# The whole depthwise convolution on TensorE, with weights spread by the host, and the weight splits of the second block on VectorE

## The chip, the cores and the metric

One core of a Trainium2 chip. TensorE (PE in the profile) multiplies and transposes, VectorE (DVE), ScalarE (ACT) and GpSimd (POOL) work element by element, SyncE (SP) issues the DMAs, 16 DMA engines move the data. The metric is device time of one execution in microseconds, the median of several runs; lower is better.

## The reference

Two transformer blocks on one sequence of 256 positions and width 1024, in float32. The first block (a hybrid attention mixer and a SwiGLU FFN, closed by an RMS norm) is not touched. The second, cut to what matters:

```python
h = rms_norm_2(x, norm1_g)
q, k, v, a, g = jnp.split(h @ w_in, splits, axis=-1)         # 512 wide each
attn = neighbourhood_attention(q, k, v, rpb)
conv = conformer_conv(a, g, conv_w, conv_b, conv_ln_g, conv_ln_b)
mixed = concat([rms_norm_2(attn, attn_out_g), rms_norm_2(conv, conv_out_g)])
x = x + mixed @ w_out
h = rms_norm_2(x, norm2_g)
x = x + expert_choice_ffn(h, w_router, w_gate, w_up, w_down) # 16 experts, 1024 -> 2048 -> 1024
return rms_norm_2(x, final_g)

def conformer_conv(a, gate, ...):
    u = a * sigmoid(gate)
    dw = depthwise_conv(u, conv_w) + conv_b    # 31 taps over positions, 512 channels, each by itself
    return silu(layer_norm(dw, ln_g, ln_b))
```

## The kernel before, in words

**Splits.** A linear layer works on float32 weights in slabs of 128x1024. `split()` (L278 on) makes of each slab a high part `wh` (ScalarE, L287) and a low part `wl` = slab minus `wh` (L288, on VectorE or, where the table `POOLS` names the slab, on GpSimd). `linear_steps()` asks for the splits of a layer and then issues, per slab and row half, six products: high with high and low, low with high, of two k each (L249). A product can't start before its `wh` or `wl` is there.

**The second block.** Five linears read `w_b[0..4]`: the first two give the GLU halves of the conv (`ev_glu(n)`; its product `th`, L963, is transposed on TensorE and copied into `upad`), then q, k and v. The out projection `w_o2` has a part for the conv (`mixC`) and, at the end, one for the attention (`mixA`). The first linear begins while the first block's last slabs leave (`leave`, tiles `raw` and `xg`). The 31 taps of the 512 channels run in four chunks of 128 channels:
- chunk 0 on VectorE, 31 operations on `acc[:, 0]` (L1008, L1010);
- chunk 1 on ScalarE (product) and GpSimd (sum, L1024);
- chunks 2 and 3 on TensorE (`conv_pe`): `upad` goes to DRAM (`udram`), comes back as `u4`, four copies of 32 channels shifted by one position (four DMAs a chunk), and 32 small products a chunk take four taps each. Their spread weights `wst` are built on the core from `conv_wq` and `sumsel`, by GpSimd and by VectorE.

`swish` then transposes `acc`, takes the LayerNorm (`BN_STATS`, `z`) and the swish, and makes `mixC`. `scores` and `values` are the attention (`e`, `pt`, `on`, `mixA`). The router and the experts follow.

**What sets the order.** Every part is a generator that yields either a time or the marks that it needs. `weave` (L233) runs the flow that is due first by a clock of its own, that counts the products issued; TensorE follows this order as written, the other engines run in the order of their queues. SP's queue issues nearly all DMAs, in order: one that waits for a slot holds all behind it.

**Loads ahead.** Twelve slots of 2 MB hold one expert's weights (`in_e_g`, `in_e_u`, `in_e_d`, some as two halves). Four `e_g` slots of the first expert load during the FFN of the first block, at the slabs in `AH`, into the pools of `turns`; the others as the second block frees them. The loads of the next expert reuse them one by one, when TensorE has read them.

Of the kernel before, what the change touches and what calls it, by code (L numbers as in the profile page):

```python
# [9 lines left out]
FT = mybir.dt.float32  # L10
# [3 lines left out]
AF = mybir.ActivationFunctionType  # L14
OP = mybir.AluOpType
# [29 lines left out]
_columns(PRM, [("iota", 32), ("nhalf", 16), ("n2_g", 8), ("fin_g", 8)])  # L45
_columns(PR2, [("sumsel", 32), ("ffn_g", 8), ("out_g", 8), ("conv_w", 62), ("conv_wq", 64), ("conv_b", 4), ("w_r", 128)])

# [10 lines left out]
def _arrays(i):  # L58
# [28 lines left out]
    put("n2_g", _cols(i["norm2_g_2"][0]))  # L87
    cw = i["conv_w_2"][0]
    put("conv_w", cw[:, :256].T.reshape(2, 128, 31).transpose(1, 0, 2))
    cw = np.concatenate([cw[:, 256:], np.zeros((1, 256), np.float32)])  # L90
    put("conv_wq", cw.reshape(8, 4, 2, 4, 32).transpose(1, 4, 2, 3, 0))
    put("conv_b", _cols(i["conv_b_2"][0]))
# [42 lines left out]

POOLS = [[], [1, 3], [1, 3], [1, 3], [1, 3], [1, 3], [1, 3], [0, 1, 3], [1, 3], [1, 3], [], [], [], [3], [3], [3], [2, 3], [3], [3], [3], [2, 3], [3], [3], [2, 3], [], [1, 3], [1, 3], [1, 3]]
AH = [2, 4, 7, 8]
ORDERS = [(0, 0, 0, 1, 0, 1, 1, 1), (0, 0, 0, 0, 1, 1, 1, 1), (0, 0, 1, 0, 0, 1, 1, 1), (0, 0, 0, 1, 1, 0, 1, 1), (0, 0, 1, 0, 1, 0, 1, 1), (0, 1, 0, 0, 1, 0, 1, 1)]
# [6 lines left out]
def _program(nc, tc, A, dbg=None):  # L145
# [84 lines left out]
    def mark(name, after=0.0):  # L230
        marks[name] = clock[0] + after
# [77 lines left out]

    def linear_steps(slot, xt, evac, n=512, gcol=None, mid=None, ks=range(8), turn=None, fine=False, pool=False):  # L310

        us = sorted({k // 2 for k in ks})
        on, order_ = (range(8), 0) if pool else next(settings)
        turn = turn or ORDERS[order_]
# [544 lines left out]

    ahead = []  # L860
    turns = [[ringh] * 2, [ringx], [ringb], [ringb]]

    def feed():
        prev = []
        for b in range(11):
# [90 lines left out]
    def ev_glu(n):  # L956
        def ev(t, ps):
# [45 lines left out]
    def conv_dve():
        yield "u00", "u01"
        for k in range(31):
            u, w = upad[:, 0, k:k + 256], cw[:, 0, k:k + 1]
            if k == 0:
                V.tensor_scalar(acc[:, 0], u, w, cb[:, 0:1], op0=OP.mult, op1=OP.add)  # L1008
            else:
                V.scalar_tensor_tensor(acc[:, 0], u, w, acc[:, 0], op0=OP.mult, op1=OP.add)  # L1010
            if k % 3 == 2:
                yield 2.48
        mark("conv0", 4.72)

    def conv_act():
        yield "u00", "u01"
        for k in range(31):
            u, w = upad[:, 1, k:k + 256], cw[:, 1, k:k + 1]
            if k == 0:
                S.activation(acc[:, 1], u, AF.Identity, bias=cb[:, 1:2], scale=w)  # L1020
            else:
                o = be.tile([128, 256], FT, tag="prod", name="prod", bufs=2)
                S.activation(o, u, AF.Identity, scale=w)
                G.tensor_tensor(acc[:, 1], acc[:, 1], o, op=OP.add)  # L1024
            if k % 3 == 2:
                yield 0
        mark("conv1", 2.96)


    udram = dram.tile([2, 128, 288], FT, name="udram")  # L1030

    def conv_pe():
        wq = pp("conv_wq").rearrange("p (c a g) -> p c a g", c=2, g=8)
        sumsel = pp("sumsel")[:, None, :].to_broadcast([128, 8, 32])
        wst = be2.tile([128, 4, 8, 32], FT, tag="wst", name="wst")
        with tc.issue_after(last_pow[0]):
            for j in range(4):
                G.tensor_tensor(wst[:, j], wq[:, 0, j, :, None].to_broadcast([128, 8, 32]), sumsel, op=OP.mult)
        yield "u10", "u11"
        for c in range(2):  # L1040
            u4 = be2.tile([128, 4, 284], FT, tag="u4", name="u4")
            for r in range(4):
                nc.sync.dma_start(out=u4[32 * r:32 * r + 32], in_=udram[c, :, r:r + 284].rearrange("(j i) s -> i j s", i=32))
            yield 8.16
            ps = bank("sc")
            for g in range(8):
                for j in range(4):
                    MM(ps[32 * j:32 * j + 32, :256], wst[:, j, g], u4[:, j, 4 * g:4 * g + 256], g == 0, g == 7)
                if g % 2:
                    yield 0  # L1050
            S.activation(acc[:, 2 + c], ps[:, :256], AF.Identity, bias=cb[:, 2 + c:3 + c])
            if c == 0:
                wst = be2.tile([128, 4, 8, 32], FT, tag="wst", name="wst")
                for j in range(4):
                    V.tensor_tensor(wst[:, j], wq[:, 1, j, :, None].to_broadcast([128, 8, 32]), sumsel, op=OP.mult)
        mark("conv2", 0.81)

# [106 lines left out]
    def block():  # L1164
# [299 lines left out]
```

## Time and profile before

| | us |
|---|---|
| median of three runs | 1457.74 |
| lowest, highest | 1454.93, 1458.69 |
| the profiled execution | 1459.36 |
| its span in the profile | 1456.6 |
| TensorE busy | 1119.6 (77%) |
| VectorE busy | 443.5 (30%) |
| GpSimd busy | 165.7 (11%) |

Times in the profile are microseconds from the start of the span. A row of the time order gives start, duration, engine, line, operation, out<-in and, in brackets, how long the engine was idle before it and what ended that. Rows that follow one another with the same names are drawn together (x18 are eighteen instructions).

### The profile page before, as it was taken

To read this page: it belongs to the slowest core of one execution; us is meant where nothing else is said; L and a number is where in the kernel's file an instruction comes from. 1 tells how busy PE (TensorE), PEld (TensorE's weight loads), DVE (VectorE), ACT (ScalarE), POOL (GpSimd) and SP (SyncE) were. 2 spreads that over 40 slices of the span, in tenths; PEclk is the share of its full clock that TensorE was granted. 3 is DMA by queue.
4 is the path that set the end of the run, shared out by engine and by line. 5 is a ranking of instruction groups with operands and counts; after the bars stand their busy time and mean duration, and the time that the engine had idled before them with its cause. 6 is when DMAs were issued, how large, how long until landed. Compare 5 with 4: busy or idle time off the path is not lost.

```text
span 1456.6 us, 15371 instructions
## 1 busy us (share of the span) xinstructions
PE 1119.6 (77%) x6323; PEld 562.7 (39%) x6323; DVE 443.5 (30%) x819; ACT 332.2 (23%) x610; POOL 165.7 (11%) x119
## 2 busy tenths in 40 slices
PE   6989999999998898765675665677666667676575
PEld 5867877888876684111211111121111121111112
DVE  6576676445589542100110010001000011011002
ACT  5455646445576631000000000000000000000001
POOL 4433200100048530000000000000000000000001
PEclk9999999999999899888788788877778878878879
DMA  8623256757454578999999999999999999999997
GB/s 299 254 107 116 87 202 238 279 209 294 165 188 146 196 296 346 427 429 429 430 429 427 430 430 428 431 427 430 431 425 430 431 428 428 428 430 429 428 429 295
DMA packets 50598, 494.65 MB, mean 340 GB/s; under 512 B 5857, under 2 KB 7649, under 8 KB 10721
## 3 DMA queue, kind: packets, MB, share of 16 engines
q1 hardware_dynamic: 50528, 493.69, 82.3%
q8 instruction: 49, 0.80, 0.2%
q14 instruction: 21, 0.16, 0.0%
HBM read 492.32 MB, written 1.34 MB: 339 GB/s over the span
## 4 chain that ended last, share of the span: by engine, by line
DMA 63%; PE 24%; DVE 9%; ACT 2%; issue 1%; SPq 0%; POOL 0%; POOLq 0%; ACTq 0%; DVEq 0%
DMA slot<-in_e_g 18%; DMA half<-in_e_d 15%; PE mm L249 14%; DMA half<-in_e_g 8%; DMA half<-in_e_u 7%; DMA slot<-in_e_u 6%; PE dn L249 4%; DMA slot<-in_e_dl 2%; DMA slot<-in_e_d 2%; DMA slot<-in_w_gu 2%; DVE acc L1010 2%; DVE wl L288 2%; PE tr L254 1%; PE sc L249 1%; DMA slot<-in_w_a 1%
## 5 line engine op out<-in xcount | busy, mean ns | idle before, releaser
L1339 PE MATMUL mm<-slot,xg 128*32 128x512 f32 x1536 | 236.9, 748 | 142.4 <-DMA slot<-in_e_u 92.2
L249 PE MATMUL mm<-wh,xt 128*128 128x512 f32 (+1 forms) x896 | 293.8, 398 | 4.9 <-DVE ropeb L446 3.3
L249 PEld LDWEIGHTS mm<-wh,xt 128*128 128x128 f32 x896 | 170.3, 191 | 44.5 <-issue 8.9
L1370 DVE TENSOR_TENSOR x<-acc,x 128x512 f32<-128x512 f32 x60 | 41.5, 692 | 455.2 <-PE acc L1368 455.2
L249 PE MATMUL mm<-wl,xt 128*128 128x512 f32 (+1 forms) x448 | 175.9, 393 | 4.1 <-DVE wl L288 3.5
L1363 PE MATMUL sc<-half,hT 128*32 128x512 f32 x720 | 127.9, 798 | 62.5 <-DMA half<-in_e_d 62.5
L1339 PEld LDWEIGHTS mm<-slot,xg 128*32 128x32 f32 x1536 | 47.6, 124 | 312.4 <-issue 123.8
L288 POOL TENSOR_TENSOR wl<-slot,wh 128x1024 fp32r<-128x1024 f32 (+1 forms) x40 | 96.8, 2424 | 229.1 <-ACT wh L287 217.3
L287 ACT ACTIVATE wh<-slot 128x1024 fp32r<-128x1024 f32 (+1 forms) x104 | 106.6, 1040 | 51.2 <-PE mm L249 40.6
L1405 POOL TENSOR_TENSOR x<-x,fing 128x256 f32<-128x256 f32 (+1 forms) x8 | 5.2, 660 | 896.9 <-ACT sq L1403 896.9
L1346 DVE TENSOR_TENSOR sil<-sil,mm 128x512 f32<-128x512 f32 x16 | 11.0, 688 | 290.3 <-PE mm L1339 290.3
L1368 PE MATMUL acc<-eo,owT 128*128 128x512 f32 x120 | 81.4, 765 | 21.8 <-DVE x L1370 11.8
L1339 PE MATMUL mm<-half,xg 128*32 128x512 f32 x512 | 74.6, 664 | 29.8 <-DMA half<-in_e_u 18.6
L288 DVE TENSOR_TENSOR wl<-slot,wh 128x1024 fp32r<-128x1024 f32 (+1 forms) x64 | 82.9, 1309 | 38.7 <-ACT wh L287 38.6
L249 PEld LDWEIGHTS mm<-wl,xt 128*128 128x128 f32 x448 | 85.7, 191 | 21.3 <-DVE wl L288 5.1
L1384 ACT ACTIVATE eo<-sc 128x512 f32<-128x512 f32 x15 | 9.0, 597 | 357.0 <-PE sc L1363 357.0
L1363 PEld LDWEIGHTS sc<-half,hT 128*32 128x32 f32 x720 | 17.6, 124 | 163.8 <-DMA half<-in_e_d 138.6
L351 DVE SCALAR_TENSOR_TENSOR wl<-slot,pr,wh 128x512 fp32r<-128x512 f32 x88 | 62.8, 765 | 47.0 <-ACT wh L350 47.0
L1359 ACT ACTIVATE owT<-tr 128x256 f32<-128x256 f32 x16 | 6.1, 383 | 298.1 <-PE tr L1357 298.1
L350 ACT ACTIVATE wh<-slot,pr 128x512 fp32r<-128x512 f32 x88 | 58.1, 715 | 47.9 <-PE mm L249 30.7
L1368 PEld LDWEIGHTS acc<-eo,owT 128*128 128x128 f32 x120 | 21.7, 227 | 92.3 <-DVE x L1370 32.2
L1345 ACT ACTIVATE sil<-mm 128x512 f32<-128x512 f32 x16 | 9.6, 597 | 192.5 <-PE mm L1339 192.5
(337 smaller groups left out, 1122.3 us busy)
## 6 DMA issues: line engine op xcount, KB each, us to landing
slot<-in_e_g SPq DMA_DIRECT2D x48, 2048.0 KB, 24.4
slot<-in_e_u SPq DMA_DIRECT2D x48, 2048.0 KB, 29.2
half<-in_e_d SPq DMA_DIRECT2D x90, 1024.0 KB, 24.4
half<-in_e_g SPq DMA_DIRECT2D x32, 1024.0 KB, 29.4
half<-in_e_u SPq DMA_DIRECT2D x32, 1024.0 KB, 31.6
slot<-in_e_d SPq DMA_DIRECT2D x15, 2048.0 KB, 29.2
slot<-in_w_gu SPq DMA_DIRECT2D x11, 2048.0 KB, 8.3
slot<-in_w_a SPq DMA_DIRECT2D x7, 2048.0 KB, 8.7
```

The lines of the kernel that those rows point to most:

```text
L249: T.matmul(out, lhsT=lhsT, rhs=rhs, start=start, stop=stop)
L254: T.transpose(out, src, ident if idn is None else idn)
L287: S.activation(h, src, AF.Copy)
L288: (G if pool else V).tensor_tensor(l, src, h.bitcast(FT), op=OP.subtract)
L350: S.activation(h, ps, AF.Identity, scale=col)
L351: V.scalar_tensor_tensor(l, ps, col, h.bitcast(FT), op0=OP.mult, op1=OP.subtract)
L1010: V.scalar_tensor_tensor(acc[:, 0], u, w, acc[:, 0], op0=OP.mult, op1=OP.add)
L1339: T.matmul(ps[32 * j:32 * j + 32], lhsT=xg[:, k, s0:s0 + 32], rhs=slot[kk][:, j * 512:(j + 1) * 512], start=k == 0, stop=k == 7)
L1346: V.tensor_tensor(sil, sil, gu[1], op=OP.mult)
L1363: T.matmul(ps[32 * j:32 * j + 32, :c.stop - c.start], lhsT=hT2[:, q * 128 + 32 * j:q * 128 + 32 * j + 32], rhs=slot[n][:, j * 512 + c.star ...
L1368: T.matmul(ps, lhsT=owT[:, t * 128:(t + 1) * 128], rhs=eo, start=True, stop=True)
L1370: V.tensor_tensor(x[:, t, k], ps, x[:, t, k], op=OP.add)
```

## The change

All four chunks of the conv go through TensorE. The host lays the taps out in spread form (`w_cv`, 128x4096, 2 MB), so that `wst`, `conv_w`, `conv_wq` and the code that built them go. `conv()` takes two chunks for each GLU half `n`, as soon as that half's `upad` is in its own `udram[n]`; eight `u4` reads for each `n`, into two buffers. `w_cv` is loaded in the FFN, at slab 4, into the pool `ringx`, where an `e_g` slot of the first expert was; that `e_g` is loaded after the conv. In the second block all entries of `POOLS` are empty, and the splits of both `w_o2` slabs go to VectorE too. `weave` gets the flows in the order conv, swish, scores, values, block.

```diff
-POOLS = [..., [], [], [], [3], [3], [3], [2, 3], [3], [3], [3], [2, 3], [3], [3], [2, 3], [], [1, 3], [1, 3], [1, 3]]
-AH = [2, 4, 7, 8]
+POOLS = [..., [], [], [], [3], [3], [3], [2, 3], [3], [3], [3], [2, 3], [3], [3], [], [], [], [], []]
+AH = [2, 7, 8]
...
-    turns = [[ringh] * 2, [ringx], [ringb], [ringb]]
+    turns = [[ringh] * 2, [ringb], [ringb], [ringx]]
...
+            if b == 4:
+                with tc.issue_after(last_load[0]):
+                    w_cv.append(load(flat(A["w_cv"]), pool=ringx))
...
-                if n and t:
-                    nc.sync.dma_start(out=udram.rearrange("c p s -> p c s"), in_=upad[:, 2:])
+                if t:
+                    nc.sync.dma_start(out=udram[n].rearrange("c p s -> p c s"), in_=upad[:, 2 * n:2 * n + 2, :288])
...
+    def conv():
+        w = w_cv[0].rearrange("p (c j g m) -> p c j g m", c=4, j=4, g=8)
+        for n in range(2):
+            yield f"u{n}0", f"u{n}1"
+            u4 = [be2.tile([128, 4, 284], FT, tag="u4", name="u4", bufs=2) for c in range(2)]
+            for c in range(2):
+                for r in range(4):
+                    nc.sync.dma_start(out=u4[c][32 * r:32 * r + 32], in_=udram[n][c, :, r:r + 284].rearrange("(j i) s -> i j s", i=32))
+            yield 13.0
+            for c in range(2):
+                ps = bank("sc")
+                for g in range(8):
+                    for j in range(4):
+                        MM(ps[32 * j:32 * j + 32, :256], w[:, 2 * n + c, j, g], u4[c][:, j, 4 * g:4 * g + 256], g == 0, g == 7)
+                    if g % 2:
+                        yield 0
+                S.activation(acc[:, 2 * n + c], ps[:, :256], AF.Identity, bias=cb[:, 2 * n + c:2 * n + c + 1])
+        mark("conv", 0.81)
...
-        yield "conv0", "conv1", "conv2"
+        yield "conv",
...
-            yield from linear_steps(w_o2[0][:, n * 2048:(n + 1) * 2048], mixC, add_scaled("c", n), ks=range(4), pool=True)
+            yield from linear_steps(w_o2[0][:, n * 2048:(n + 1) * 2048], mixC, add_scaled("c", n), ks=range(4), own=[])
...
-    flows = (swish(), values(), scores(), conv_pe(), conv_dve(), conv_act(), block())
-    weave(*(flows[i] for i in [3, 0, 2, 1, 4, 5, 6]))
+    weave(conv(), swish(), scores(), values(), block())
...
-    hl = [[split(w_o2[1][...], 1024, pool=[1, 1, 1, 1][2 * n + u]) for u in range(2)] for n in range(2)]
+    hl = [[split(w_o2[1][...], 1024, pool=[0, 0, 0, 0][2 * n + u]) for u in range(2)] for n in range(2)]
```

TensorE, from the products of the v linear ahead of the last conv chunk to the transposes of the conv sums (`acc`); `xt` is the block's input, `u` with a number a chunk's shifted copies, `qk` an output of the q or k linear. Before:

```order
L249 MATMUL mm<-wh,xt 128x512
L249 MATMUL sc<-u_3987,wst 32x256 x32
L254 MATMUL tr<-fst,qk 128x128 x4
L249 MATMUL mm<-wh,xt 128x512
L249 MATMUL mm<-wl,xt 128x512
L249 MATMUL mm<-wh,xt 128x512 x2
L249 MATMUL mm<-wl,xt 128x512
L249 MATMUL mm<-wh,xt 128x512
L254 MATMUL acc<-fst,acc 128x128 x4
L249 MATMUL sc<-kT,qT 128x256 x4
```

After:

```order
L250 MATMUL mm<-wh,xt 128x512
L250 MATMUL sc<-u_3840,slot 32x256 x32
L250 MATMUL sc<-u_3841,slot 32x256 x32
L250 MATMUL mm<-wh,xt 128x512
L250 MATMUL mm<-wl,xt 128x512
L250 MATMUL mm<-wh,xt 128x512 x2
L250 MATMUL mm<-wl,xt 128x512
L250 MATMUL mm<-wh,xt 128x512
L255 MATMUL acc<-fst,acc 128x128 x4
```

Two chunks stand in a row where one stood (`slot` is `w_cv`), and the same is found once more ahead, behind the second GLU half's last products; one group of six products follows the conv ahead of the transposes, as before.

VectorE, from the last GLU product to the LayerNorm of the conv. Before:

```order
L963 SCALAR_TENSOR_TENSOR th<-th,ga 128x256
L1010 SCALAR_TENSOR_TENSOR acc<-upad,pr_105,acc 128x256 x9
L288 TENSOR_TENSOR wl<-slot,wh 128x1024
L1010 SCALAR_TENSOR_TENSOR acc<-upad,pr_105,acc 128x256 x7
L288 TENSOR_TENSOR wl<-slot,wh 128x1024
L1010 SCALAR_TENSOR_TENSOR acc<-upad,pr_105,acc 128x256 x2
L1055 TENSOR_TENSOR wst<-pr_105 128x256 x4
L288 TENSOR_TENSOR wl<-slot,wh 128x1024 x2
L1087 BN_STATS smalls<-acc 128x6
```

After:

```order
L967 SCALAR_TENSOR_TENSOR th<-th,ga 128x256
L289 TENSOR_TENSOR wl<-slot,wh 128x1024 x8
L1055 BN_STATS smalls<-acc 128x6
L1056 BN_AGGR smalls<-smalls 128x2
L378 TENSOR_SCALAR smalls<-smalls 128x1
L289 TENSOR_TENSOR wl<-slot,wh 128x1024
L1055 BN_STATS smalls<-sc 128x6
L1059 TENSOR_SCALAR z<-acc,smalls 128x512
```

The taps and the `wst` products are gone, eight splits stand where four were, and one more split has come between the two halves of the LayerNorm. At the start of the block, not shown, three splits stand between the last two `raw` and `xg` of the first block.

SP's queue, from the load of the attention's bias to the last halves of the first expert (`in_w_o` is the out projection). Before:

```order
L215 DMA slot<-in_bias 128x4096
L1043 DMA u_3987<-udram 32x4x284 x4
L215 DMA slot<-in_w_o 128x4096
L215 DMA slot<-in_e_u 128x4096 x2
L215 DMA slot<-in_w_o 128x4096
L215 DMA slot<-in_e_u 128x4096
L1192 DMA tri<-in_tri 128x128
L805 DMA half<-in_e_u 128x2048 x2
L215 DMA slot<-in_e_d 128x4096
L805 DMA half<-in_e_d 128x2048 x6
```

After:

```order
L216 DMA slot<-in_bias 128x4096
L216 DMA slot<-in_e_g 128x4096
L216 DMA slot<-in_w_o 128x4096
L216 DMA slot<-in_e_u 128x4096
L216 DMA slot<-in_w_o 128x4096
L216 DMA slot<-in_e_u 128x4096
L216 DMA slot<-in_e_d 128x4096
L1159 DMA tri<-in_tri 128x128
L216 DMA slot<-in_e_u 128x4096
L806 DMA half<-in_e_u 128x2048 x2
L806 DMA half<-in_e_d 128x2048 x6
```

The `e_g` that gave way to `w_cv` comes behind the bias; the `u` reads are ahead of it; and `e_d`'s slot, that waits for the last split of the second `w_o` slab, has moved ahead of the last `e_u` slot and of the two `e_u` halves.

## Rows read from the trace of the kernel before

**Rows 1.** From the page: the span, and the chain that ended last by engine.

```profile
span 1456.6 us, 15371 instructions
DMA 63%; PE 24%; DVE 9%; ACT 2%; issue 1%; SPq 0%; POOL 0%; POOLq 0%; ACTq 0%; DVEq 0%
```

**Rows 2.** Busy time by stretches: length, busy time of each engine, granted TensorE clock, share of the 16 DMA engines, GB/s.

```profile
435.00:465.00 30.00, 23.36 (x148) 17.55 (x146) 29.40 (x28) 17.49 (x32) 24.06 (x20) 0.94 0.31 101
555.00:557.00 2.00, 1.74 (x13) 1.77 (x13) 1.02 (x4) 0.00 (x0) 0.00 (x0) 0.83 0.06 20
563.00:1400.00 837.00, 559.28 (x3208) 132.59 (x3204) 80.49 (x147) 24.85 (x47) 0.00 (x0) 0.81 1.01 429
```

(The busy times are of PE, its weight loads, DVE, ACT and POOL, in this order.)

**Rows 3.** The chain of waits in order of time around the start of the experts: start, duration, what it went through.

```profile
555.26 2.80 PE tr L1297 x16
...
568.41 14.79 DMA slot<-in_e_g
```

**Rows 4.** What PE waited for from 417 to 556 us: total, times, longest.

```profile
PE tr L254 <- DVE th L963: 3.8, 1, 3.8
PE tr L254 <- DVE z L1097: 3.3, 1, 3.3
PE mm L249 <- DVE wl L288: 2.7, 1, 2.7
PE sc L249 <- DMA u<-udram: 2.4, 2, 2.0
...
PE mm L249 <- DVE mixa L345: 0.8, 1, 0.8
```

**Rows 5.** PE in order of time: GLU transposes (`th`), the linears' products, transposes of q and k (`qk`), the conv chunks (`u,wst`), score products (`kT,qT`), transposes of `z`, first product of the out projection.

```profile
428.78 0.38 PE L254 MATMUL tr<-fst,th 128*128 128x128 f32 x2
...
439.81 0.44 PE L254 MATMUL tr<-fst,th 128*128 128x128 f32 x2 [3.83 <-DVE th L963]
...
445.81 0.38 PE L254 MATMUL tr<-fst,th 128*128 128x128 f32 x2
...
451.88 0.48 PE L249 MATMUL mm<-wh,xt 128*128 128x512 f32 x1
...
456.10 0.60 PE L254 MATMUL tr<-fst,qk 128*128 128x128 f32 x4
...
458.52 3.66 PE L249 MATMUL sc<-u,wst 128*32 128x256 f32 x64 [0.43 <-DMA u<-udram]
...
477.41 5.35 PE L249 MATMUL sc<-u,wst 128*32 128x256 f32 x64 [2.00 <-DMA u<-udram]
...
485.10 1.14 PE L249 MATMUL sc<-kT,qT 64*128 64x256 f32 x8
...
498.98 1.09 PE L254 MATMUL tr<-fst,z 128*128 128x128 f32 x4 [3.30 <-DVE z L1097]
...
506.31 0.39 PE L249 MATMUL mm<-wh,mixc 128*128 128x512 f32 x1
```

**Rows 6.** Groups of instructions of DVE and of POOL from 417 to 535 us: line, engine, operation, count | busy time, mean ns of one | idle time ahead.

```profile
L1010 DVE SCALAR_TENSOR_TENSOR acc<-upad,pr,acc 128x256 f32<-128x256 f32 x30 | 27.6, 921 | 0.9
L288 DVE TENSOR_TENSOR wl<-slot,wh 128x1024 fp32r<-128x1024 f32 x10 | 15.6, 1568 | 2.5 <-ACT wh L287 2.5
...
L580 DVE COPY pt<-tr 128x512 f32<-128x512 f32 x4 | 2.8, 689 | 3.9 <-PE tr L254 3.9
...
L1146 DVE TENSOR_TENSOR on<-acc,smalls 128x512 f32<-128x512 f32 x2 | 1.4, 692 | 5.7 <-PE acc L249 5.7
...
L288 POOL TENSOR_TENSOR wl<-slot,wh 128x1024 fp32r<-128x1024 f32 x14 | 34.7, 2479 | 10.9 <-ACT wh L287 10.8
```

**Rows 7.** DVE in order of time, single operations.

```profile
411.62 1.90 DVE L939 TENSOR_TENSOR smalls<-smalls 128x1 f32<-128x1 f32 x1
...
414.88 2.03 DVE L834 TENSOR_TENSOR xg<-raw,gb 128x512 f32<-128x512 f32 x1
...
422.01 0.57 DVE L939 TENSOR_TENSOR smalls<-smalls 128x1 f32<-128x1 f32 x1 [0.66 <-POOL smalls L378]
...
442.45 1.22 DVE L288 TENSOR_TENSOR wl<-slot,wh 128x1024 fp32r<-128x1024 f32 x1
...
485.21 0.70 DVE L1087 BATCH_NORM_STATS2 smalls<-acc 128x6 f32<-128x512 f32 x1 [9.48 <-PE acc L254]
...
488.99 0.67 DVE L1093 TENSOR_TENSOR z<-z,ln 128x512 f32<-128x512 f32 x1
...
493.19 2.82 DVE L1093 TENSOR_TENSOR z<-z,ln 128x512 f32<-128x512 f32 x1
...
498.15 0.68 DVE L1097 SCALAR_TENSOR_TENSOR z<-th,z 128x512 f32<-128x512 f32 x1
```

**Rows 8.** SP's queue in order of time: reads of the shifted copies of `u`, the slot of the first expert's `e_d`, the first load of the next expert.

```profile
449.17 2.05 SPq L1043 DMA_DIRECT2D u<-udram  x4
...
532.99 0.33 SPq L215 DMA_DIRECT2D slot<-in_e_d  x1
...
559.96 1.19 SPq L805 DMA_DIRECT2D half<-in_e_g  x2
```

**Rows 9.** The tile `u` (the shifted copies): its DMA issues, with the nanoseconds that an issue takes, and the time from issue to landing.

```profile
L1043 SPq DMA_DIRECT2D u<-udram x8: 303/478/820, 449.2 to 467.5; - x8
...
DMA to landing us min/median/max: 7.7/8.9/10.2
```

More of the change, by code (lines that the diff above doesn't have):

```diff
@@ L45 @@
 _columns(PRM, [("iota", 32), ("nhalf", 16), ("n2_g", 8), ("fin_g", 8)])
-_columns(PR2, [("sumsel", 32), ("ffn_g", 8), ("out_g", 8), ("conv_w", 62), ("conv_wq", 64), ("conv_b", 4), ("w_r", 128)])
+_columns(PR2, [("sumsel", 32), ("ffn_g", 8), ("out_g", 8), ("conv_b", 4), ("w_r", 128)])
 def _blocks(w, width):
@@ L87, in _arrays @@
     put("n2_g", _cols(i["norm2_g_2"][0]))
[L88 to L91, printed above, removed]
+    cw = np.concatenate([i["conv_w_2"][0], np.zeros((1, 512), np.float32)]).reshape(8, 4, 4, 4, 32).transpose(1, 4, 2, 3, 0)
+    wide = np.zeros((4, 32, 4, 4, 8, 32), np.float32)
+    for c in range(32):
+        wide[:, c, :, :, :, c] = cw[:, c]
+    out["w_cv"] = wide.reshape(128, 4096)
     put("conv_b", _cols(i["conv_b_2"][0]))
@@ L133, in _arrays @@
     return {n: np.ascontiguousarray(a) for n, a in out.items()}
-POOLS = [[], [1, 3], [1, 3], [1, 3], [1, 3], [1, 3], [1, 3], [0, 1, 3], [1, 3], [1, 3], [], [], [], [3], [3], [3], [2, 3], [3], [3], [3], [2, 3], [3], [3], [2, 3], [], [1, 3], [1, 3], [1, 3]]
-AH = [2, 4, 7, 8]
+POOLS = [[], [1, 3], [1, 3], [1, 3], [1, 3], [1, 3], [1, 3], [0, 1, 3], [1, 3], [1, 3], [], [], [], [3], [3], [3], [2, 3], [3], [3], [3], [2, 3], [3], [3], [], [], [], [], []]
+AH = [2, 7, 8]
 ORDERS = [(0, 0, 0, 1, 0, 1, 1, 1), (0, 0, 0, 0, 1, 1, 1, 1), (0, 0, 1, 0, 0, 1, 1, 1), (0, 0, 0, 1, 1, 0, 1, 1), (0, 0, 1, 0, 1, 0, 1, 1), (0, 1, 0, 0, 1, 0, 1, 1)]
@@ L308, in flush, with linear_steps @@
             posts.pop(0)[1]()
-    def linear_steps(slot, xt, evac, n=512, gcol=None, mid=None, ks=range(8), turn=None, fine=False, pool=False):
+    def linear_steps(slot, xt, evac, n=512, gcol=None, mid=None, ks=range(8), turn=None, fine=False, own=None):
         us = sorted({k // 2 for k in ks})
-        on, order_ = (range(8), 0) if pool else next(settings)
+        on, order_ = next(settings) if own is None else (own, 0)
         turn = turn or ORDERS[order_]
@@ L858, in down @@
             flush(clock[0])
-    ahead = []
-    turns = [[ringh] * 2, [ringx], [ringb], [ringb]]
+    ahead, w_cv = [], []
+    turns = [[ringh] * 2, [ringb], [ringb], [ringx]]
     def feed():
@@ L970, in post @@
                 mark(f"u{n}{t}", 1.0)
-                if n and t:
-                    nc.sync.dma_start(out=udram.rearrange("c p s -> p c s"), in_=upad[:, 2:])
-                    mark("udram", 3.0)
+                if t:
+                    nc.sync.dma_start(out=udram[n].rearrange("c p s -> p c s"), in_=upad[:, 2 * n:2 * n + 2, :288])
             later(2.42 if n else 1.88, post)
@@ L999, in _program @@
     acc = be.tile([128, 4, 256], FT, tag="acc", name="acc")
-    cw = pp("conv_w").rearrange("p (c k) -> p c k", c=2)
     cb = pp("conv_b")
[L1003 to L1027, printed above, removed]
@@ L1030, in _program @@
[L1030 to L1056, printed above, removed]
@@ new lines, in _program @@
+    udram = [dram.tile([2, 128, 288], FT, name=f"udram{n}") for n in range(2)]
+    def conv():
[16 more added lines that the diff above has]
+        mark("conv", 0.81)
@@ L1227, in ev_h3 @@
         later(0.92, post)
-    hl = [[split(w_o2[1][:, n * 2048 + u * 1024:n * 2048 + (u + 1) * 1024], 1024, pool=[1, 1, 1, 1][2 * n + u]) for u in range(2)] for n in range(2)]
+    hl = [[split(w_o2[1][:, n * 2048 + u * 1024:n * 2048 + (u + 1) * 1024], 1024, pool=[0, 0, 0, 0][2 * n + u]) for u in range(2)] for n in range(2)]
     for n in range(2):
```

## The prediction, before the result was known

> **What bounds the kernel now.** Read the page first: of the chain that ended last, 63% is DMA and 24% TensorE [rows 1]. The next view, busy time by stretches, shows why. From 563 us to 1400 us the 16 DMA engines are busy all the time at 429 GB/s, while TensorE runs at a granted clock of 0.81 and still waits [rows 2]: the weights of sixteen experts stream in, and nothing there goes faster than they do. Ahead of that stands a hole: from 555 to 557 us the DMA moves 20 GB/s [rows 2]. All twelve slots are full with expert 0, and the next load may start only when TensorE has read a first slot. The chain of waits says the same: TensorE, PE, starts the experts at 555.26, and from 568.41 the chain is slot loads alone [rows 3]. The first new load is issued at 559.96 [rows 8].
>
> So the end is (first released slot) + (fifteen experts by DMA) + (a tail that the change leaves alone). The change edits the second block, ahead of the experts, where PE is the path. A microsecond saved on PE between 417 and 555 moves the end by a microsecond, as long as expert 0 is fully loaded by then. Hence the third view, what PE waits for there [rows 4], and its instructions in order of time [rows 5].
>
> **What it removes.** VectorE, DVE, is why PE waits: it is busy 29.40 of the 30 us from 435 to 465 [rows 2], with the 30 taps of conv chunk 0 (27.6 us at 921 ns) and ten weight splits at 1568 ns [rows 6].
> 1. Waits of PE: 3.8 for the GLU product th, 3.3 for z, 2.7 for the split wl, 2.4 for u, 0.8 for mixa [rows 4]; 13.0 in all. I take each as gone in its present form; what is late next is an addition below.
> 2. The clock that falls after them: over 435 to 465 the granted clock is 0.94 [rows 2], full but for stretches at the lower of its two levels, 1.2 GHz, right behind a wait. The second pair of GLU transposes to the next takes 6.00 (439.81 to 445.81) for 18 products; another 18 products with their transposes take 4.22 (451.88 to 456.10) [rows 5]. With 0.15 for two transposes that is 1.6 lost. Conv chunk 3, straight after its own wait, takes 5.35, chunk 2 takes 3.66: 1.7 lost. From the z transposes at 498.98 to the first mixc product at 506.31 it is 7.33; at the rate of the full stretches it is 0.4 for the transposes, 1.1 for eight score products (485.10) and 2.8 for twelve products at 0.234: 4.3, so 3.0 lost [rows 5]. Sum 6.3.
> Removed: **19.3 us.**
>
> **What it adds.**
> 3. Two more chunks on PE, 64 instructions each at the form and count of those of before: 2 x 3.66 = 7.3 [rows 5]. Ends: 3.66 (at full clock) and 5.35 (behind a wait) each.
> 4. The start. All splits are DVE's now, and in the new order three stand ahead of the last xg, on which the first transposes of the block wait: at 1.2 each (442.45, [rows 7]) 3.6. On the other side GpSimd, POOL, is silent. While it splits, DVE's operations stretch: a [128,1] product took 1.90 at 411.62 and 0.57 at 422.01, and xg took 2.03 at 414.88 where a product of the same 128x512 takes 0.67 (488.99) [rows 7]. That returns 1.3 + 1.4 = 2.7. Net +0.9 (ends 0 and 3.6).
> 5. A smaller z wait. From the statistics at 485.21 to the end of z at 498.83 DVE needs 13.6 [rows 7]; one z product of 2.82 becomes 0.67 with POOL silent, one split of 1.2 now lies between: 12.6. In the new order PE has between the transposes that start this and those that wait for it some 10.9 us of its own work. A wait of about 1.5 to 1.7; I take 1.5 (ends 0 and 3.3, the wait of before).
> 6. The clock behind that wait: 0 to 1.7, I take 0.9 (half of what conv chunk 3 lost).
> 7. The tail of the attention. The mixc products are issued earlier, and the last pt, on and gx have less beside them. Three copies at 0.69 [rows 6]: 2.0 (ends 0 and 2.1).
> Added: 7.3 + 0.9 + 1.5 + 0.9 + 2.0 = **12.6 us.** Net 6.7.
>
> **What is costed at nothing, and by what it is hidden.** The u reads: before, the last GLU transposes (445.81) are followed by the first u read at 449.17 [rows 8], 3.4 later, and a read lands 8.9 us (at most 10.2) after its issue [rows 9]. The first half's transposes move from 428.78 to some 429.7 with term 4, so its eight reads are issued from 433.1 to 437.2 (four take 2.05) and the first chunk's land by 444.8, the second's by 447.4. PE gets there at 439.81 - 3.83 + 0.9 = 436.9 for the third transposes, 18 products later (441.1) for the fourth, 18 more later for the chunk: 445.5, and 3.66 later for the next: 449.2. Hidden by 0.7 and 1.8 us: just so. The second half has 60 products between, and its reads have landed before.
> The taps' weights w_cv (2.1 MB): loaded in the FFN in place of a slot of expert 0, which goes after the conv instead; from 435 to 465 the DMA runs at 101 GB/s [rows 2], so there is room. POOL's 14 splits at 2479 ns become DVE's at about 1.2; DVE loses 27.6 us of taps [rows 6] and has the room.
> The loads of expert 0: SyncE's queue, SP, runs in order, and e_d's slot now stands in front of one e_u slot and all the halves. It waits for the last split of the second w_o slab: 532.99 before [rows 8]; in the new order the split stands before the last pt copy and runs on the faster engine, and I estimate 517 (at worst 525, the old time less 6.7 and 1.2). Behind it lie 12.6 MB, 29.3 us at 429 GB/s: landed by 546, at worst 554, while PE's first release moves from 559.96 to 553. Hidden by 7 us, at worst missed by 1.
>
> **A rule that says otherwise.** By the rows a read of 32 partitions (four make a chunk, 145 KB each) lands after 7.7 to 10.2 us [rows 9], and the change doubles the number of reads. The Trainium skill, "DMA: Bandwidth & Descriptors", section "Anatomy of one DMA", gives a DMA a fixed cost of about 2.0 us and its bytes at 436 GB/s, by which a read would land in some 2.3 us (an estimate from that page), the cover would be 7 us and rival (a) would fall. The rows say four times that, so the chance of (a) goes by the rows.
>
> **The rivals.**
> (a) *Late reads or a slow clock in the conv.* The cover is 0.7 us. If the first pair of chunks waits 2.00 as chunk 3 did and both then run in 5.35 [rows 5], that is 2.0 + 3.4 = 5.4 back: 1458.1 on the profiled scale, 1456 as a median. For: chunks 2 and 3 both waited before. Against: their reads were issued 9.4 us ahead, these 12. Chance 0.16; no change.
> (b) *DVE's order.* Eight w_o splits and one of w_b now stand among the z and mixc operations; if two of them are ahead of z, its wait is 3.5 and the clock behind it falls for 3.0, as before: 1.5 + 0.9 become 6.5, +4.1: 1455. For: DVE runs in order and a split waits for ScalarE's half. Against: 12.6 against 10.9 above. Chance 0.09; no change.
> (c) *Slower: the queue behind e_d.* Everything of expert 0 behind e_d's slot starts with its release G. From G + 29.3 later than 553, that is G later than 523.7, each microsecond costs one: at 531 the gain is gone, and at 536 the end is 1463 or later. For: the old gate is 532.99. Against: the split moves to an engine that does it in half the time and is asked earlier. Chance 0.07; slower.
> (d) *The added bytes land on the bound.* If the slot of expert 0 that gave way is not loaded in the idle stretch, 2.1 MB at 429 GB/s are 4.9 us on the DMA: 1456. Against: 101 GB/s there. Chance 0.03; no change.
>
> **How the numbers follow.** The profiled run took 1459.36 around its span of 1456.6; the median of the three runs is 1457.74, 1.6 less. 1459.4 - 6.7 = 1452.7, as a median **1451.1**. The forecast has 0.65. Its terms 4 to 7 together span -5 to +6, seldom all one way; I take 1445 to 1456 for it. With (a), (b), (d) at 1455 to 1456 inside and (c) mostly left out, the range is 1444 to 1458. A measurement can tell about 0.3%, 4.4 us: faster is below 1453.4, slower above 1462.1. The forecast gives faster 0.60 and same 0.05; (a), (b), (d) give same 0.27 and slower 0.01; (c) gives slower 0.07. Faster 0.60, same 0.32, slower 0.08.
>
> **What would show it.** Right: no wait of PE for th or wl between 417 and 500; conv as four groups of about 3.66; DVE with ten or so idle microseconds between 435 and 465; a z wait of 1 to 2; the experts' first transposes at 547 to 550, the first new load at 552 to 555, and the hole in the DMA narrower but there. Wrong: a wait of the conv for u (a), a z wait over 3 with half-speed products behind it (b), e_d's slot issued after 524 and no hole in the DMA (c). If the experts start at 548 and the end has not moved with them, the claim that PE's path sets the end is what failed.

## The result, and the profile after

| | before | after |
|---|---|---|
| median, us | 1457.62 (4 runs, 1454.93 to 1458.69) | 1447.15 (4 runs, 1446.61 to 1447.60) |
| profiled execution, us | 1459.36 | 1446.61 |
| its span, us | 1456.6 | 1444.8 |

The ratio is 0.9931, with a 95% interval of 0.9914 to 0.9948: 10.5 us faster. Measured once more, the changed kernel stood at 1448.21 beside 1457.99 (0.9932, 0.9915 to 0.9949). The forecast was 1451.1, 6.7 less than before.

The page of the changed kernel, to be read against [rows 1]: the span and the chain that ended last by engine.

```profile
span 1444.8 us, 15517 instructions
DMA 59%; PE 32%; DVE 5%; ACT 2%; issue 1%; POOL 0%; SPq 0%; POOLq 0%; ACTq 0%; DVEq 0%
```

Busy time by stretches, columns as in [rows 2]; the 547 row is the stretch ahead of the first new load.

```profile
435.00:465.00 30.00, 30.00 (x237) 22.81 (x236) 9.99 (x9) 13.77 (x19) 0.00 (x0) 1.00 0.73 225
...
547.00:549.00 2.00, 2.00 (x14) 0.46 (x17) 0.42 (x1) 0.00 (x0) 0.00 (x0) 0.50 0.21 82
...
563.00:1400.00 837.00, 557.52 (x3154) 130.62 (x3146) 83.36 (x150) 24.86 (x47) 0.00 (x0) 0.81 1.01 429
```

From 435 to 465 TensorE is busy all 30 us at full clock, where it was 23.36 at 0.94; VectorE has fallen from 29.40 to 9.99, GpSimd is silent. The expert stage is as it was, 429 GB/s, and the hole ahead of it has shrunk but is there.

What PE waited for from 417 to 546 us, against [rows 4], and PE in order of time, against [rows 5].

```profile
PE tr L255 <- DVE z L1065: 1.9, 1, 1.9
...
PE tr L255 <- DVE on L1114: 0.8, 1, 0.8
PE tr L255 <- DVE gx L1038: 0.7, 1, 0.7
PE acc L250 <- DVE pt L581: 0.4, 1, 0.4
```

```profile
434.84 0.38 PE L255 MATMUL tr<-fst,th 128*128 128x128 f32 x2
...
439.19 0.38 PE L255 MATMUL tr<-fst,th 128*128 128x128 f32 x2
...
443.63 7.11 PE L250 MATMUL sc<-u,slot 128*32 128x256 f32 x128
...
465.87 7.11 PE L250 MATMUL sc<-u,slot 128*32 128x256 f32 x128
...
487.74 0.63 PE L255 MATMUL tr<-fst,z 128*128 128x128 f32 x4 [1.91 <-DVE z L1065]
488.30 1.13 PE L250 MATMUL sc<-kT,qT 64*128 64x256 f32 x8
489.37 0.50 PE L250 MATMUL mm<-wh,xt 128*128 128x512 f32 x1
```

The waits for th, wl, u and mixa are gone, and so is the slow stretch behind th: 4.35 us from 434.84 to 439.19, where it was 6.00. Two chunks take 7.11 on the clock, with no wait in front. What is left is 1.9 for z and three short waits in the attention's tail (for `on`, for `gx`, from which mixa is made, and for `pt`); the router's two behind them (1.5 for aff, 0.8 for oh) were there before as well.

SP's queue, against [rows 8], and the tile `u`, against [rows 9].

```profile
426.23 0.33 SPq L216 DMA_DIRECT2D slot<-in_w_b  x1
428.61 0.39 SPq L976 DMA_DIRECT2D udram<-upad  x1
435.77 3.66 SPq L1014 DMA_DIRECT2D u<-udram  x8
...
515.92 0.33 SPq L216 DMA_DIRECT2D slot<-in_e_d  x1
...
549.23 1.23 SPq L806 DMA_DIRECT2D half<-in_e_g  x2
```

```profile
L1014 SPq DMA_DIRECT2D u<-udram x16: 302/430/432, 435.8 to 452.1; - x16
...
DMA to landing us min/median/max: 2.3/3.4/4.3
```

The first new load is issued at 549.23 where it was 559.96, 10.7 us earlier. A read of u lands in 2.3 to 4.3 us, not in the 7.7 to 10.2 of before: of that below. There it matters what stood in the queue just ahead of the first reads, which [rows 8] leave out:

```profile
446.64 0.39 SPq L972 DMA_DIRECT2D udram<-upad  x1
447.13 0.41 SPq L215 DMA_DIRECT2D slot<-in_w_b  x1
```

**How the runs are compared.** The part of the program ahead of the edits scatters by itself. So positions are counted here from the last pairs of transposes of the first block's hidden tile (`hid`, TensorE, the first pair after 390 us), in each kernel's own profile:

| kernel | hid at | to third th | to first mixc | to the experts | experts to the end |
|---|---|---|---|---|---|
| before | 399.86 | 39.95 | 106.45 | 155.40 | 901.3 |
| changed | 398.53 | 36.31 | 96.35 | 146.05 | 900.2 |
| changed, once more | 400.72 | 36.62 | 96.67 | 146.60 | 901.5 |
| conv alone | 398.85 | 36.24 | 95.67 | 147.65 | 900.4 |
| splits alone | 400.27 | 38.74 | 102.23 | 151.42 | 901.5 |
| an eighth of the conv | 400.24 | 36.67 | 86.15 | 137.31 | 900.1 |
| load ahead of u | 396.78 | 36.33 | 106.91 | 156.69 | 900.1 |
| one chunk on VectorE | 400.87 | 36.49 | 92.81 | 144.55 | 901.6 |
| the same, once more | 400.58 | 36.14 | 92.41 | 143.81 | 900.0 |
| and the cast on GpSimd | 397.59 | 36.26 | 92.55 | 142.36 | 901.3 |
| scores behind z | 397.49 | 36.78 | 101.23 | 152.48 | 901.5 |
| second group behind z | 397.13 | 36.44 | 96.25 | 146.99 | 902.1 |
| chunk, scores behind z | 399.30 | 36.55 | 97.52 | 148.76 | 901.3 |
| chunk, second group behind z | 399.02 | 36.37 | 92.43 | 144.56 | 901.6 |

The last column is the span less the experts' start. Over a range of some 18 us in that start (537.55 to 555.26) it stays within 2.1: the end follows the start of the experts one for one. The first column scatters by 4.1 us over kernels whose program is the same up to there, or nearly so. Of the 10.7 us by which the experts start earlier in the profile, 9.35 are therefore the change's (8.8 in its second profile), the rest is where the two executions happened to stand. The kernel before has one profile only, so how far its own column scatters is not known. One execution of it beside the first four experiments, at 3418 us, is left out of their ratios.

### The profile page after: what moved, and what is told of

The parts are those of the page before. It is cut to its first block, busy times and chain, and to the rows that moved or that the text cites. A ratio compares the mean times of both kernels' runs of the same rounds, so it can differ in the third digit from the quotient of the medians.

```text
span 1444.8 us, 15517 instructions
## 1 busy us (share of the span) xinstructions
PE 1118.9 (77%) x6451; PEld 562.5 (39%) x6451; DVE 419.9 (29%) x800; ACT 320.7 (22%) x581; POOL 94.7 (7%) x69
## 3 DMA queue, kind: packets, MB, share of 16 engines
HBM read 495.52 MB, written 1.64 MB: 344 GB/s over the span
## 4 chain that ended last, share of the span: by engine, by line
DMA 59%; PE 32%; DVE 5%; ACT 2%; issue 1%; POOL 0%; SPq 0%; POOLq 0%; ACTq 0%; DVEq 0%
DMA half<-in_e_d 20%; PE mm L250 19%; DMA half<-in_e_u 18%; DMA slot<-in_e_g 8%; DMA slot<-in_e_u 4%; DMA half<-in_e_g 4%; PE dn L250 4%; PE mm L1306 3%; DMA slot<-in_e_dl 2%; PE sc L250 2%; PE tr L255 2%; DVE wl L289 1%; DMA slot<-in_w_a 1%; DMA half<-in_e_dl 1%; ACT wh L288 1%
## 5 line engine op out<-in xcount | busy, mean ns | idle before, releaser
L1330 PE MATMUL sc<-half,hT 128*32 128x512 f32 x720 | 125.0, 780 | 65.5 <-DMA half<-in_e_d 65.4
L289 DVE TENSOR_TENSOR wl<-slot,wh 128x1024 fp32r<-128x1024 f32 (+1 forms) x80 | 99.1, 1249 | 65.5 <-ACT wh L288 64.9
L289 POOL TENSOR_TENSOR wl<-slot,wh 128x1024 fp32r<-128x1024 f32 (+1 forms) x24 | 57.0, 2375 | 217.2 <-ACT wh L288 205.5
```

The lines of the kernel that those rows point to most:

```text
L289: (G if pool else V).tensor_tensor(l, src, h.bitcast(FT), op=OP.subtract)
L1330: T.matmul(ps[32 * j:32 * j + 32, :c.stop - c.start], lhsT=hT2[:, q * 128 + 32 * j:q * 128 + 32 * j + 32], rhs=slot[n][:, j * 512 + c.star ...
```

## The experiments

**The two halves of the change, each alone.** The conv on TensorE, but the splits shared with GpSimd as before:

```diff
-POOLS = [..., [3], [3], [], [], [], [], []]
+POOLS = [..., [3], [3], [2, 3], [], [1, 3], [1, 3], [1, 3]]
...
-  ... mixC, add_scaled("c", n), ks=range(4), own=[])
+  ... mixC, add_scaled("c", n), ks=range(4), own=range(8))
...
-  ... pool=[0, 0, 0, 0][2 * n + u] ...
+  ... pool=[1, 1, 1, 1][2 * n + u] ...
```

> The changed kernel with the splits of the second block shared with GpSimd as before (the conv part of the change alone). Theory A, the taps on VectorE were the load that made TensorE wait: the wait for th stays gone (under 1 us), the z operations are stretched again to 2 us and more while GpSimd splits, so the z wait is 3 to 5 us; e_d's slot, that waits for the last split, is issued 4 to 8 us later than the 515.9 of the changed kernel, so the hole in the DMA closes. Experts start 3 to 5 us after the 544.6 of the changed kernel; 1449 to 1453 us. Rival B, GpSimd's splits and the stretch that they put on VectorE were the cause: most of the 10.5 us are lost, 1454 us and above.

Measured: 1449.03 beside 1457.19 (0.9944, 0.9929 to 0.9959), 8.2 us faster. Its wait for z, and the gate of e_d:

```profile
PE tr L255 <- DVE z L1065: 1.3, 1, 1.3
```

```profile
517.47 0.33 SPq L216 DMA_DIRECT2D slot<-in_e_d  x1
```

Theory A's time held, at the lower end of its range; its details did not. The z wait is shorter than in the changed kernel, not longer (the split that stood between the two halves of the LayerNorm is GpSimd's here); the z product beside GpSimd takes 1.34 at most, not 2 and more; the gate is 1.6 us later, not 4 to 8; and the experts start 1.9 later, not 3 to 5. Counted from the hid transposes that is 1.05 to 1.6, and up to the first mixc product the path is even shorter than in the changed kernel; 1.5 us of the loss are the clock's, behind the on transposes (below).

The splits on VectorE, but the conv as before (the reverse of the diff, in the kernel before):

> The kernel before with all splits of the second block on VectorE and the conv as it was (the other part alone). Theory A: VectorE has no room (29.4 of 30 us busy from 435 to 465); some seven more splits of 1.2 us stand in its queue up to 485, less what GpSimd's silence returns; the waits of TensorE for th, wl and z grow by 4 to 10 us together: 1460 to 1468 us. Rival B: taps and splits get so much shorter without GpSimd (taps from 921 to 500 ns, splits from 1568 to 1220) that TensorE's waits shrink: 1450 to 1456 us.

Measured: 1454.64 beside 1457.19 (0.9978, 0.9967 to 0.9989), 2.6 us faster. Groups of VectorE from 417 to 500 us, and what PE waited for:

```profile
L1010 DVE SCALAR_TENSOR_TENSOR acc<-upad,pr,acc 128x256 f32<-128x256 f32 x30 | 24.9, 831 | 0.7
L288 DVE TENSOR_TENSOR wl<-slot,wh 128x1024 fp32r<-128x1024 f32 x18 | 23.9, 1336 | 1.9 <-ACT wh L287 1.8
...
L963 DVE SCALAR_TENSOR_TENSOR th<-th,ga 128x256 f32<-128x256 f32 x4 | 2.4, 602 | 0.0
```

```profile
PE tr L254 <- DVE z L1097: 4.4, 1, 4.4
PE tr L254 <- DVE th L963: 2.2, 1, 2.2
...
PE sc L249 <- DMA u<-udram: 1.5, 1, 1.5
...
PE mm L249 <- DVE wl L288: 0.8, 1, 0.8
```

Theory A fell here, rival B held: VectorE took eight more splits and TensorE waited less (8.9 us for th, z, wl and u, 12.2 before), since VectorE's operations got shorter with GpSimd's splits gone. Taps went from 921 to 831 ns, splits from 1568 to 1336, th from 950 to 602 ([rows 6] for the first two). Only z, behind the added splits, is later. The two halves add up within their intervals: 8.2 + 2.6 = 10.8 for 10.5 measured together.

**Does the end follow TensorE's path?** Only the first of eight tap groups is computed:

```diff
-                for g in range(8):
+                for g in range(1):
...
```

> The changed kernel with only one of the eight tap groups of each chunk: 16 products of a chunk's 128 records in place of all, seven eighths of the convolution are left out. TensorE's path to the experts loses 14.1 x 7/8 = 12.3 us. Theory A, the path of TensorE sets the end one for one, and the gate of the first expert's loads moves with it: experts start at 532 to 534 and the time is 1434 to 1438 us. Rival C, the loads of the first expert already are the next bound (the hole in the DMA is only 2 us wide): the end moves by 2 to 4 us, 1443 to 1445 us.

Measured: 1438.63 beside 1457.19 (0.9876, 0.9856 to 0.9896); 8.5 under the changed kernel. Up to the first mixc product the path is 10.2 shorter, up to the experts 8.7. So neither number: the path sets the end (900.1 behind the experts), but the path didn't shrink by all of the 12.3. Two things took some back. The chain of waits shows one:

```profile
507.43 0.33 SPq L216
507.76 0.05 issue
507.81 8.02 DMA tri<-in_tri
515.89 0.11 issue
515.99 0.75 DVE x L1171
```

The small triangle table is queued behind e_d's slot and lands 8 us after its issue. VectorE's conversion of it stands in order ahead of the first sum of x, and TensorE waits 1.1 us for that x. The other is the clock, 0.95 from 465 to 500, where it was 1.00. It fell behind the wait for z, which is as long as in the changed kernel:

```profile
477.69 0.63 PE L255 MATMUL tr<-fst,z 128*128 128x128 f32 x4 [1.91 <-DVE z L1065]
478.25 1.38 PE L250 MATMUL sc<-kT,qT 64*128 64x256 f32 x8
479.56 0.80 PE L250 MATMUL mm<-wh,xt 128*128 128x512 f32 x1
```

The product takes 0.80 where it took 0.50, and from these transposes to the first mixc product it is 8.70, where it was 7.14: 1.6 lost. Rival C fell: at the hole of 2 us the loads were not the bound, since the gate moved along (507.43 for 515.92).

**What sets the landing of a small read?** The 2 MB load of the last w_b goes ahead of the first eight reads of u:

```diff
+            if n == 0:
+                w_bs.extend(load(flat(A["w_b"][i])) for i in (2, 3, 4))
+            with tc.issue_after(last_load[0]):
                 for c in range(2):
                     for r in range(4):
                         nc.sync.dma_start(out=u4[c]..., in_=udram[n][c, ...])
```

> The changed kernel with the 2 MB load of the last w_b put in the queue ahead of the first eight reads of u, behind them before. Those reads landed in 2.3 to 4.3 us in the changed kernel and in 7.7 to 10.2 in the kernel before. Theory D, a small read waits for the big load that is ahead of it in the queue: issued from 440 on they land 7 to 11 us later, TensorE waits 4 to 7 us at the first chunk and the clock may fall behind that: experts 4 to 8 us later, 1451 to 1456 us. Rival E, the size or the DRAM round trip sets it: they land in 2.3 to 4.3 us, TensorE waits 1 to 2 us, 1447 to 1450 us.

Measured: 1458.83 beside 1457.19 (1.0014, 1.0003 to 1.0024), slower than the changed kernel by 11.7 and than the kernel before by 1.6. SP's queue, the landing of the tile u, and PE:

```profile
437.99 0.34 SPq L216 DMA_DIRECT2D slot<-in_w_b  x1
438.38 10.16 SPq L1019 DMA_DIRECT2D u<-udram  x8
```

```profile
DMA to landing us min/median/max: 2.5/3.8/10.5
```

```profile
450.69 5.66 PE L250 MATMUL sc<-u,slot 128*32 128x256 f32 x68 [8.72 <-DMA u<-udram]
```

Theory D holds: with the same size and the same DRAM round trip, the seven reads right behind the 2 MB land 10.1 to 10.5 us after their issue, the eight of the second half 2.5 to 3.2. (The kernel with one chunk on VectorE, below, shows it without being made for it: 2.6 to 3.1 for the reads of its first half, 7.5 to 8.0 for the four issued right behind a load of w_b.) The Trainium skill, "DMA: Bandwidth & Descriptors", section "Queues, rings and completion order", says that each DMA engine takes a queue's descriptors in the order of the ring; the trace agrees, 10.5 against 2.5 us. The price is larger than expected, since the load itself goes out late and holds the reads: counted from the hid transposes the first is issued at 41.60, at 37.24 in the changed kernel. (The 10.16 us of the eight issues have a pause of 6.1 in them, but ahead of the eighth, which the first chunk doesn't need.) The profile is that of the fastest of ten executions, 1455.42.

**What else VectorE could do.** Score operations behind the last z operation:

```diff
+                  with (tc.issue_after(zf[1]) if len(zf) == 2 else nullcontext()):
                     V.tensor_tensor_reduce(out=e4[:, h], ...
```

> The changed kernel with VectorE's score operations of the later groups queued behind the last z operation. Theory: the z wait of 1.9 us is DVE's order (four score operations, 1.5 us, stand ahead of the last z product), not work: the wait falls to 0.3 to 1.0 us and the experts start 0.9 to 1.6 us earlier, 1445.5 to 1446.5 us. Rival: ScalarE's exponentials wait for the postponed operations and the score banks come free later, so TensorE waits as long at the next score products: within 0.5 us of the changed kernel, 1446.7 to 1447.7 us.

Measured: 1453.31 beside 1457.99 (0.9963, 0.9948 to 0.9978), 5.1 slower than the changed kernel beside it. The edit caught the first group too, so the wait moved from z to the score products, which need that group's banks:

```profile
PE sc L250 <- DVE smalls L1094: 2.7, 1, 2.7
```

With the second group alone behind z (`if (t, g) == (0, 1)`):

> As the earlier edit of z, but only the second group's score operations on VectorE stand behind the last z operation (the earlier edit had caught the first group's too, whose banks the next score products need). Theory: the z wait falls from 1.9 to 0.3 to 1.0 us and no wait takes its place; from the last hidden transposes to the experts 145.0 to 145.7 us against 146.0 and 146.6 in the two profiles of the changed kernel; 1445.5 to 1447 us. Rival: the score banks come free later all the same, a wait for them of over 1 us, 1447 us and above.

Measured: 1449.39 beside 1456.44 (0.9949, 0.9937 to 0.9962). The z wait is 1.3, but a wait of 0.8 for the sum of x is new, and from the hidden transposes to the experts it is 146.99: nothing gained. What z won, other work lost.

One chunk back on VectorE, now without GpSimd beside it (`conv_dve` as in the kernel before for chunk 0, one chunk fewer in `conv` for n = 0):

```diff
-            u4 = [be2.tile(...) for c in range(2)]
+            u4 = {c: be2.tile(...) for c in (range(2) if n else [1])}
...
-            for c in range(2):
+            for c in u4:
                 ps = bank("sc")
...
+    weave(conv(), swish(), scores(), values(), conv_dve(), block())
```

> The changed kernel with the first of the four chunks back on VectorE (31 taps, interleaved as before), three on TensorE, all splits on VectorE, GpSimd silent. Theory F, GpSimd at work doubled VectorE's operations: a tap takes 0.40 to 0.48 us (0.92 in the kernel before, 0.83 with the splits alone moved), the 31 are 13 us, VectorE has the room (10 of 30 us busy from 435 to 465 in the changed kernel), and TensorE's path loses one chunk of 3.5 us: 1443 to 1445 us. Rival G, the taps are slow by themselves or stand in VectorE's queue ahead of th and wl: TensorE waits 2 us and more for these, 1447 us or above.

Measured: 1448.44 beside 1457.99 (0.9932, 0.9917 to 0.9947), no different from the changed kernel beside it, 1448.21. Groups of VectorE from 417 to 500 us:

```profile
L1034 DVE SCALAR_TENSOR_TENSOR acc<-upad,pr,acc 128x256 f32<-128x256 f32 x30 | 14.5, 483 | 0.8
```

So theory F is right about the tap, 483 ns for 921, and the path to the first mixc product is 3.9 shorter, but the time came out as rival G had it, for another reason: TensorE waits neither for th nor for wl. The loss is later, at the on transposes: first the changed kernel's second profile, then this one.

```profile
521.97 0.65 PE L255 MATMUL tr<-fst,on 128*128 128x128 f32 x4 [0.78 <-DVE on L1114]
522.38 0.48 PE L250 MATMUL mm<-wh,mixa 128*128 128x512 f32 x1
```

```profile
518.25 1.11 PE L256 MATMUL tr<-fst,on 128*128 128x128 f32 x4 [0.79 <-DVE on L1127]
519.02 0.78 PE L251 MATMUL mm<-wh,mixa 128*128 128x512 f32 x1
```

Behind the same wait (0.78 and 0.79) the same four transposes take 0.65 and 1.11: the clock fell in one (0.57 from 518 to 520, most of it at the lower level of 1.2 GHz), and from there to the first transposes of x it is 6.24 for 4.63. The same fall shows in three more profiles (the conv alone, and both kernels with all scores behind z), at 1.4 to 1.5 us; in the eight others with this wait the clock stays full. Whether the moment or the program decides was the next question.

> The kernel with one chunk on VectorE once more. Theory: the 1.6 us that it lost behind the on transposes are the clock's and belong to the place of those waits in time; if they hang on the program, the granted clock falls there again and the experts stand at 144.3 to 144.9 after the hidden transposes; if on the moment, it stays full and they stand at 142.7 to 143.2. 1444 to 1448.5 us.

Measured: 1446.20 beside 1456.44 (0.9927, 0.9911 to 0.9942). The granted clock stayed at 1.00 from 500 to 535: with the same program it fell once and once it did not. The experts stand at 143.81, since now TensorE waits 1.0 for x, for the cause seen in the eighth of the conv: VectorE idles 1.31 for the triangle table. That operation moved to GpSimd:

```diff
-    V.tensor_copy(trib[:, 0], tri)
+    G.tensor_copy(trib[:, 0], tri)
```

> The kernel with one chunk on VectorE, and the conversion of the small triangle table, that waits for its DMA behind e_d's 2 MB, on GpSimd instead of VectorE. In the second profile of the kernel with the chunk VectorE idled 1.31 us for that DMA ahead of the first sum of x, and TensorE then waited 1.0 for x. Theory: that wait is an operation in order on VectorE that nobody needs yet; without it the experts stand at 142.6 to 143.1 us after the hidden transposes (143.8 in that profile), 1443.5 to 1446.5 us. Rival: the triangle is needed as early, or VectorE is held by GpSimd's operation: 143.8 and more.

Measured: 1443.36 (1442.85 to 1445.36) beside 1455.87 (0.9914, 0.9901 to 0.9928): faster than the kernel before and than each run of the changed kernel (1446.61 at least). The experts start at 142.36. No wait for x is among those of PE.

The chunk and the z edits together, in both forms:

> The two edits of this call together (one chunk on VectorE, and z ahead of the later score operations). If both theories hold, their gains add, 3.5 and 1.2 us: 1442 to 1444 us. If only the first does, 1443 to 1445 us.

> This edit and the first chunk back on VectorE. Up to the first mixc product the path is 92.8 us with the chunk moved alone and 96.4 to 96.7 in the changed kernel; here 91.5 to 92.5. Theory: if the clock doesn't fall behind the on transposes, the experts stand at 141.5 to 142.5 after the hidden transposes, 1442 to 1445 us; if it falls as with the chunk alone (1.6 us), at 143 to 144, 1444 to 1447 us.

Measured: 1451.02 beside 1457.99 (0.9948, 0.9933 to 0.9963) with all groups behind z, the same 2.7 us wait for the banks in it; 1446.72 beside 1456.44 (0.9936, 0.9922 to 0.9951) with the second group alone, where mixc stands at 92.43, x waits 1.1 for the triangle, and the experts come at 144.56. The z edit adds nothing to the chunk.

The changed kernel once more, for the scatter of the start:

> The changed kernel once more, beside these on the same chip: 1446 to 1448 us. The part of the trace ahead of the edit (the first block's last hidden transposes) shows how far this start scatters by itself; theory: by 1 to 2 us between executions, so that of the 10.7 us by which the experts start earlier 1.3 are not the change's.

Measured: 1448.21 beside 1457.99, just above its range; hid at 400.72 for 398.53, 2.2 us apart with the same program.

## Why the prediction was right, and where its sizes were off

**The bound** held: the end stands 900.0 to 902.1 us behind the start of the experts in the fourteen profiles of the table, and a shorter TensorE path brought it nearer, a longer one (the load ahead of u) moved it away.

**Terms 1 and 2**, what is removed, held where they can be read singly. From the hidden transposes to the third th the path is 3.64 and 3.33 shorter (2.9 forecast: the wait of 3.8 less term 4), from there to the fourth 1.65 and 1.64 (1.6 forecast). The 3.0 for the clock behind z was a little too much: the changed kernel takes 4.59 for the same transposes, score products and products at full clock, where the forecast put 4.3; that makes 2.7.

**The additions were too large**, by some 2 of the 10.6 us up to the first mixc product and by a few tenths behind it. The path to mixc shrank by 10.1 and 9.8; the sum of the steps up to there is 7.9.
- Term 4, the start: 0.9 forecast, 0.33 and 0.64 measured at the first th.
- Term 3: the pairs take 7.04 from start to start of what follows, 14.1 for four chunks; four at the 3.66 of the forecast are 14.6.
- Term 5: z waits 1.9, forecast 1.5. Here the forecast was too kind.
- Term 6, the slower clock behind that wait, came out at an end of its range: 0 to 1.7, 0.9 taken, nothing paid in either profile of the changed kernel (the granted clock is 1.00 from 465 to 535). That is luck, not a rule: in the eighth of the conv the clock fell behind the same wait of 1.91 and cost 1.6, and with that the gain would have been 7.2 to 7.8, near the 6.7 of the sum.
- Some 0.4 is a group of score products that was slow before (1.51) and isn't now (1.13). A few tenths are left open.
- Term 7: the tail is longer by 0.75 and 0.98; forecast 1.2 (2.0, less the mixa wait of 0.8).

Together 9.35 or 8.8 for 6.7. The 10.5 of the medians has an interval of 7.6 to 12.5 us, and both lie in it.

Of the signs that the forecast named, two lay outside: the experts' first transposes came at 544.6 (547 to 550 forecast), the first new load at 549.2 (552 to 555). VectorE idled 20 us from 435 to 465, not ten or so.

**The reads of u** were hidden, as forecast, but by two errors that met. They were issued 2.7 us later than forecast (435.8), because the write of upad itself had the 2 MB load of 426.23 ahead of it in the queue (7.2 us from its issue to that of the reads; 2.5 before, from 446.64 to 449.17, with no load just ahead; the reads are issued as soon as the write has landed, 7.1 us after its issue), and they landed in 2.3 to 4.3 us, not 8.9. The row that was taken for the price of a small read [rows 9] was that of a read behind 2 MB. The Trainium skill, "DMA: Bandwidth & Descriptors", section "Anatomy of one DMA", from which the forecast had its estimate of 2.3 us, is written for DMAs that GpSimd issues, and these are SyncE's; the measurement with a free queue, 2.3 to 4.3, agrees with the estimate at its lower end. The forecast set it aside for the rows, and for a free queue it was the better figure. Rival (a) did not come about. The load-ahead kernel shows what would have brought it, a load in front of the reads: 8.7 us of waiting.

**The gate of e_d** came at 515.9 (517 forecast), the hole in the DMA stayed (82 GB/s in its 2 us), rival (c) did not come about. But its cover was far thinner than forecast: the last e_d half lands at 548.60, not at 546, and the first new load is issued at 549.23, not at 553, so 0.6 us were left of 7 (0.4 in the second profile, 4.1 before). In the eighth of the conv the gate moved along with the path, and 1.3 us were left. Rival (b), VectorE's order at z, shows in small: 1.9. Rival (d) did not: the slot was issued at 473 in a stretch with room.

**Why VectorE was late before** was told only in half. Its taps were a load, but half of their time was GpSimd's doing: 483 ns alone, 831 beside GpSimd's sums, 921 beside its sums and splits. The kernel before shows it by itself, VectorE first, then GpSimd:

```profile
437.20 2.56 DVE L963 SCALAR_TENSOR_TENSOR th<-th,ga 128x256 f32<-128x256 f32 x1
...
443.59 0.48 DVE L1010 SCALAR_TENSOR_TENSOR acc<-upad,pr,acc 128x256 f32<-128x256 f32 x1
443.99 0.42 DVE L963 SCALAR_TENSOR_TENSOR th<-th,ga 128x256 f32<-128x256 f32 x1
```

```profile
436.96 2.52 POOL L288 TENSOR_TENSOR wl<-slot,wh 128x1024 fp32r<-128x1024 f32 x1
439.44 1.77 POOL L1024 TENSOR_TENSOR acc<-acc,prod 128x256 f32<-128x256 f32 x2
444.60 2.45 POOL L288 TENSOR_TENSOR wl<-slot,wh 128x1024 fp32r<-128x1024 f32 x1 [3.39 <-ACT wh L287]
```

While GpSimd idles, from 441.2 to 444.6, a tap takes 0.48 and th 0.42. The th for which TensorE waited 3.83 us took 2.56 and ended at 439.76, 0.3 behind GpSimd's split. The Trainium skill, "SBUF — State Buffer", section "SBUF: two separate sides", says that GpSimd and a VectorE operation with two inputs in SBUF share one pair of ports, which whichever starts first holds for its whole instruction; the traces agree (that th; 1.22 us a split alone, up to 1.77 beside GpSimd; the [128,1] product of [rows 7], 1.90, takes 0.16 with GpSimd silent). That a chunk fits on VectorE once GpSimd is quiet was not in the forecast, and with the small conversion moved off VectorE it gave the fastest kernel here.

## What to carry to other kernels

Find the stage in which the engine waits that the end hangs on, and price an edit by that path, from mark to mark in one profile rather than from the median. Before an operation is moved off a full engine, ask whether it is full of work or stretched by its neighbour. The duration of a small transfer in a trace includes what is ahead of it in the queue; look there before taking it as its price. And an operation on a small table, ready late, holds all that stands behind it in order.

## What was not expected of the hardware

TensorE's clock does not follow from the length of a wait. In the kernel before it fell behind waits of 3.83, 3.30 and 2.00 us and stayed full behind one of 2.71. Behind a wait of 1.9 for z it stayed full in three profiles (the changed kernel twice, the load ahead of u) and fell in one (the eighth of the conv). Behind the wait of 0.78 or 0.79 for on it fell in four profiles of twelve, at 1.4 to 1.6 us each, and with the same program, one chunk on VectorE, in one execution and not in another. What decides it stays open here.
